# Attention of layer 1 with full-height low-part scores, one burst of value products per unit, and an order of TensorE written in the source

## The chip, the cores and the metric

The kernel runs on one core of one Trainium2 chip. The metric is the device time of one execution in microseconds (us). Five engines run beside each other, each with its own instruction queue: TensorE (PE in the profile, with its weight loads shown as PEld), VectorE (DVE), ScalarE (ACT), GpSimd (POOL) and SyncE (SP, which here only issues transfers). A difference of about 0.2% is the least that a measurement of this kernel can tell from none.

## The reference, cut to what matters

The reference is two transformer blocks in a row, on 512 tokens of width 1024. The first has two layers; the second of these, layer 1, is a windowed attention with 16 query heads of 64 features and 4 heads of keys and values, in which each tile of 128 queries sees its own tile, its neighbours and 256 context keys. The second block has a gated recurrence and a second, banded attention with 8 heads, and then two feed-forward parts. The lines on which the change bears are these:

```python
s_loc = jnp.einsum('bqhgd,bkhd->bhgqk', qb, kb).astype(jnp.float32) * scale
s_loc = jnp.where(valid, s_loc, NEG_INF)
s_ctx = jnp.einsum('bqhgd,bkhd->bhgqk', qb, k_ctx).astype(jnp.float32) * scale
p = jax.nn.softmax(jnp.concatenate([s_loc, s_ctx, s_sink], axis=-1), axis=-1)
return (jnp.einsum('bhgqk,bkhd->bqhgd', p_loc, vb)
        + jnp.einsum('bhgqk,bkhd->bqhgd', p_ctx, v_ctx))
...
scores = jnp.einsum('bnqhd,bnkhd->bnhqk', qc, kb) * (B_HD ** -0.5)
```

Everything is in float32, and the result is held to float32 accuracy.

## The kernel before

**Precision.** Most matrix products are made from operands that are split into a high part and a low part (`split`, L213: ScalarE casts the high part, VectorE or GpSimd subtracts it). A product then takes three passes in the fast matmul type, high by high, high by low and low by high (`mm3`, `gemm_T`, `gen_T`; all of them record on L157). The products of the probabilities with the values and the transposes run on plain float32 (L164 and L169).

**Layer 1.** The attention is cut into 16 units: a part `g` of the queries (four heads, two of each of two key heads) by a tile `i` of 128 queries. A unit goes through four stages:

- `unit_a` (L865) makes the scores. `score` writes one head: a product of the stacked queries `[hi; lo]` with the keys' high part, which `k_stack` has copied to both halves of the partitions, so that 128 rows are used, and then a product of the queries' high part alone (64 rows) with the keys' low part (64 rows of `kxl` or `kcl`). VectorE then adds the mask and takes the maximum (`evac`, L885), and ScalarE takes the exponentials. The scores of an inner tile (`mid`) lie in `sc` (256 context keys, two heads) and `sl` (384 keys of the window); those of an outer tile in one `sl` of 512.
- `trans` (L937) transposes one tile of 128 keys of the four heads on TensorE (`pt`), and ScalarE copies it to SBUF (`pr`).
- `link` (L947) adds one tile of keys to the unit's output `O`. Each product is issued as two halves of 64 output rows (`mm2`, L162), one for each half of the array's columns. With the first tile, four more such halves spread the reciprocal sums (`esk`). With the last tile, VectorE and ScalarE multiply by the gate and split the result (`yt`, `ybh`, `ybl`).
- Between these, `F.pace` issues independent work of TensorE, the fill: the projections of queries and gates (`gt`, L157), in the second half of the units the output product of the first token tiles (`gn`) and the first projections of block 2 (`pn`).

**What sets the order.** The driver (from L1106) walks over `links`, the 72 pairs of a unit and a key tile. Scores run `TL + 5 + SLACK` links ahead and transposes `TL` = 3 links ahead, and each link is followed by 1.0 to 1.2 us of fill (`FP`). This is the order in which the instructions are issued to a scheduler, which then sets the final order of each engine by priorities (`tc.high_priority`) and by when it expects operands to be ready. Only SP's queue is held to the order of the source (`manual_schedule`). Two halves of one product may so be separated by fill.

**Keys.** `k_stack` makes four transfers of 64 rows for each pair of key heads, issued on SP by `move`. They stand in SP's queue between the loads of weights (L234), and the load of the mask (`bmask`) stands behind them. The later `later(us, fn)` issues something once about so much more work of TensorE has been issued.

**Bands.** `band_a` (L1308) scores a head of the second block's banded attention in the same manner: eight products, high parts of 128 rows and low parts of 64 rows (`bk`, `bkl`, to `bS`) by turns, on keys which `band_stack` (L1147) has split and stacked.

**Pools.** PSUM is one pool of eight banks. `SLOTS` gives the number of SBUF tiles of 2 KB per partition under each tag. 24 results are written to DRAM through GpSimd's own queue (`keep`, L676).

Of the kernel before, what the change touches and what calls it, by code (L numbers as in the profile page):

```python
# [9 lines left out]
ALU = mybir.AluOpType  # L10
AX = mybir.AxisListType
P = 128
# [6 lines left out]
SLOTS = {'u': 34, 't': 13, 'p': 7}  # L19
# [3 lines left out]
# Projections of queries and gates for the attention of layer 1 in the order of need: part of the columns,  # L23
# from 4 on for the second half of the tokens.
# [79 lines left out]
def body(tc, I, out, WB=4, RB=4, LOOK=3, RA=2, TL=3, SLACK=1, NA=2, FP=(1.0, 1.2, 1.15, 3.3), HP=(30, 30, 30, 0), BW=(0.64, 0.63, 1.71, 1.5)):  # L104
# [56 lines left out]
    def mm2(ps, l, r, start, stop):  # L161
        """Two products of 64 rows each, in the two column halves of the array at once."""  # L162
# [22 lines left out]
    def settle(fill=None):  # L185
        """Issue all that was put off, with independent work in between as long as there is any."""
# [82 lines left out]
    def gemm_T(w, xparts):  # L269
        """w: per-k (hi, lo) of [128, 128 features]; xparts: (per-k (hi, lo), n) -> psum [128, n]."""  # L270
# [13 lines left out]
    def gen_T(w, xparts, evac, g=2):  # L284
        """gemm_T in steps of g contraction chunks."""
# [13 lines left out]
    class Fill:  # L299
        """Steps of independent tensor work, taken in order between the links of a latency-bound chain."""  # L300
# [17 lines left out]
        def pace(self, us):  # L318
            """Steps worth us of tensor work, less what earlier ones went beyond."""
# [13 lines left out]
    def pause(us):  # L333
        """Lets a chain of this length pass while the main stream goes on."""
# [40 lines left out]
    def ada_rows(b):  # L375
        """Layer 0: shift and scale of chunks 2b, 2b + 1 for cond and cond_ctx, as rows; even k above, odd k below."""
# [29 lines left out]
    def ada_acc(l, nb, conds, fin):  # L406
        """cond @ w for 512 columns as a sum over partitions of what the vector engine adds up, in steps of a slab."""
# [48 lines left out]
    def h_chunks(b, a):  # L456
        """(1 + scale) * x + shift for chunks 2b, 2b + 1; a: [shift | 1 + scale, chunk, cond | cond_ctx]."""
# [102 lines left out]
    def y_ahead(n):  # L560
        """Splits of y for the output product, by pass over its rows and chunk."""
# [63 lines left out]
    def ln_half(ps, gate, res, o, st, h):  # L625
        """o <- ALPHA * res + gate * ps for half h of a token tile; its statistics into st."""
# [149 lines left out]
    def k_stack(z, ks):  # L776
        """ks[e] <- [hi; hi] of head e of a pair, from the pair's hi."""
# [859 lines left out]
```

## Time and profile before

| | |
|---|---|
| median of 3 runs | 1845.38 us (1844.33 to 1846.56) |
| span of the profiled execution | 1844.1 us |
| TensorE busy | 1807.3 us, 98% of the span |
| VectorE busy | 984.6 us, 53% |
| ScalarE busy | 683.9 us, 37% |
| GpSimd busy | 185.2 us, 10% |
| stage of layer 1's units, first score to last value product | 660.8 to 972.4 us |
| stage of the bands, first score to last value product | 1091 to 1274 us |

An engine's busy time is the time in which the profiler shows an instruction on it. Matmuls are pipelined, so the length of one record of TensorE (its second column in the timeline) overlaps with the next; what one costs in a row of them is the distance from its start to the start of the next, and that is how the timeline's rows are used here. A plain float32 product leaves two records, so a row that says x2 is one instruction and x4 is two. TensorE's clock has two levels, 2.4 GHz (1.00 in the column PEclk) and 1.2 GHz (0.50).

### The profile page before, as it was taken

The page shows a single profiled execution, that of the slowest core. Times are in us where ns is not written, and L with a number is a line of the kernel's source. Part 1 is how long each engine was busy: PE and PEld are TensorE (multiplying, and loading weights), DVE is VectorE, ACT ScalarE, POOL GpSimd, SP SyncE. Part 2 cuts the span into 40 slices and gives each one's busy share as a digit, 9 for nine tenths or more (in the row PEclk, how much of TensorE's full clock was granted, in tenths as well). Part 3 has the DMA queues.
Part 4 walks back from the last instruction along what each step waited for, and adds up shares of the span by engine and source line. Part 5 has one row for each costly group of instructions (what it writes and reads, how often), then busy time and mean ns, then how long its engine had stood idle before and what let it go on. Part 6 is the DMA issues. An engine that isn't in the chain of part 4 may idle for free. (4 is left out here: it accounts for less than half of the span.)

```text
span 1844.1 us, 24591 instructions
## 1 busy us (share of the span) xinstructions
PE 1807.3 (98%) x9728; PEld 1455.2 (79%) x9728; DVE 984.6 (53%) x1782; ACT 683.9 (37%) x1275; POOL 185.2 (10%) x144
## 2 busy tenths in 40 slices
PE   8999999999999999999999899999999999999998
PEld 5788888888778987666667777778888888888887
DVE  2335676555565886555666765774445333332253
ACT  2322222222434355455454555423234332322152
POOL 1000000000000221112023611221001000000000
PEclk9999999999999999999999999999999999999999
DMA  8312343324445451222135563211244323233331
GB/s 282 130 57 80 103 142 122 115 92 131 147 148 174 134 160 58 69 81 69 64 109 160 172 205 98 69 63 58 92 136 145 107 93 102 93 99 105 110 99 69
DMA packets 66996, 209.31 MB, mean 114 GB/s; under 512 B 9152, under 2 KB 10176, under 8 KB 66880
## 3 DMA queue, kind: packets, MB, share of 16 engines
q1 hardware_dynamic: 64960, 201.45, 33.8%
q0 software_dynamic: 1920, 6.29, 0.9%
q8 instruction: 76, 1.25, 0.3%
q14 instruction: 40, 0.33, 0.1%
HBM read 195.65 MB, written 8.39 MB: 111 GB/s over the span
## 5 line engine op out<-in xcount | busy, mean ns | idle before, releaser
L214 ACT CAST hi<-raw 128x1024 fp32r<-128x1024 f32 x284 | 298.8, 1053 | 618.1 <-issue 168.4
L215 DVE TENSOR_TENSOR lo<-raw,hi 128x1024 fp32r<-128x1024 f32 x236 | 292.8, 1244 | 360.6 <-ACT hi L214 357.9
L215 POOL TENSOR_TENSOR lo<-raw,hi 128x1024 fp32r<-128x1024 f32 x48 | 117.8, 2459 | 303.0 <-ACT hi L214 302.6
L157 PE MATMUL gt<-hnhl,hi 128*128 128x512 f32 (+1 forms) x384 | 142.7, 372 | 0.2 <-DVE hnhl L199 0.2
L157 PE MATMUL gt<-hnhh,hi 128*128 128x512 f32 (+1 forms) x384 | 142.7, 372 | 0.1
L365 POOL TENSOR_TENSOR rstd<-vr,mhalf 128x1 f32<-128x1 f32 (+2 forms) x40 | 38.6, 966 | 1036.9 <-DVE vr L208 1033.3
L157 PE MATMUL gt<-hnhh,lo 128*128 128x512 f32 (+1 forms) x384 | 142.4, 371 | 0.0
L157 PE MATMUL gt<-hxhh,hi 128*128 128x512 f32 x256 | 104.3, 408 | 0.0
L157 PE MATMUL gt<-hxhh,lo 128*128 128x512 f32 x256 | 101.6, 397 | 0.0
L157 PE MATMUL gt<-hxhl,hi 128*128 128x512 f32 x256 | 101.2, 395 | 0.0
L157 PE MATMUL gt<-h2hh,hi 128*128 128x512 f32 x224 | 90.5, 404 | 0.0
L157 PE MATMUL gt<-h2hh,lo 128*128 128x512 f32 x224 | 87.5, 390 | 0.0
L157 PE MATMUL gt<-h2hl,hi 128*128 128x512 f32 x224 | 87.4, 390 | 0.0
L157 PE MATMUL gt<-h1hh,hi 128*128 128x256 f32 x288 | 86.4, 300 | 0.0
L157 PE MATMUL gt<-h1hl,hi 128*128 128x256 f32 x288 | 85.0, 295 | 0.0
L157 PE MATMUL gt<-h1hh,lo 128*128 128x256 f32 x288 | 83.7, 291 | 0.0
L157 PEld LDWEIGHTS gt<-hnhh,hi 128*128 128x128 f32 x384 | 72.3, 188 | 12.9 <-DVE hnhh L659 0.3
L157 PEld LDWEIGHTS gt<-hnhl,hi 128*128 128x128 f32 x384 | 72.3, 188 | 12.7 <-DVE hnhl L199 0.4
L157 PEld LDWEIGHTS gt<-hnhh,lo 128*128 128x128 f32 x384 | 72.3, 188 | 12.5
L202 DVE SCALAR_TENSOR_TENSOR z<-z,gt 128x256 f32<-128x256 f32 (+1 forms) x48 | 23.3, 505 | 105.8 <-ACT z L211 105.8
L157 PE MATMUL gt<-lc,hi 128*128 128x256 f32 x256 | 71.7, 280 | 0.0
L157 PE MATMUL gt<-hc,lo 128*128 128x256 f32 x256 | 71.6, 280 | 0.0
(373 smaller groups left out, 4205.1 us busy)
## 6 DMA issues: line engine op xcount, KB each, us to landing
raw<-ada_w SPq DMA_DIRECT2D x32, 512.0 KB, 4.4
raw<-a_o SPq DMA_DIRECT2D x32, 512.0 KB, 3.9
raw<-w_fg SPq DMA_DIRECT2D x22, 512.0 KB, 3.8
raw<-w_fu SPq DMA_DIRECT2D x22, 512.0 KB, 3.7
raw<-w_fd SPq DMA_DIRECT2D x22, 512.0 KB, 3.7
raw<-ada SPq DMA_DIRECT2D x16, 512.0 KB, 5.2
raw<-a_v SPq DMA_DIRECT2D x16, 512.0 KB, 4.2
raw<-a_u SPq DMA_DIRECT2D x16, 512.0 KB, 3.8
```

The costliest lines, as they stand in the source:

```text
L157: nc.tensor.matmul(ps, l, r, start=start, stop=stop)
L202: nc.vector.scalar_tensor_tensor(o, a, s, b, op0=o0, op1=o1)
L214: nc.scalar.copy(hi, src)
L215: (eng or nc.vector).tensor_tensor(lo, src, f(hi), op=ALU.subtract)
L365: nc.gpsimd.tensor_tensor(r, t, mhalf[:, :w], op=ALU.pow)
```

## The change

- `k_stack` now stacks the low parts as well as the high parts: a pair of key heads has four stacked tiles (`ks`) and eight transfers, where there were two tiles and four transfers. `score` and `band_a` make the second product over all 128 rows, the stacked queries `[hi; lo]` with `[lo; lo]`; so the product of low by low is now added too.
- In an inner tile, `unit_a` issues the scores of both heads, context and window, before it issues their evacuation.
- `link` becomes `burst`: the four `esk` halves and all of a unit's products with the values are issued without anything between.
- The driver walks over units. Within `manual_schedule` for TensorE it issues, for unit n, the burst, and then the transposes of unit n + 1 and the four steps of the scores of unit n + 2, each followed by an equal share of `FU` = 6.2 us of fill. TensorE's queue keeps this order from the first unit to the last; the other engines are still ordered by the scheduler.
- `SLOTS` grows from 34 to 38 tiles of tag `u` and from 7 to 8 of tag `p`; `dynamic_dma_scratch_size`, the SBUF set aside for GpSimd's queue of transfers, is set to 4096 bytes per partition.
- Comments are replaced by empty lines; up to L775 the line numbers stay the same.

```diff
-SLOTS = {'u': 34, 't': 13, 'p': 7}
+SLOTS = {'u': 38, 't': 13, 'p': 8}
...
-    def k_stack(z, ks):
-        for e, r in enumerate((lo_half, hi_half)):
-            for d in (lo_half, hi_half):
-                move(ks[e][d, :], z[r, :])
+    def k_stack(zs, kk):
+        for z, ks in zip(zs, kk):
+            for e, r in enumerate((lo_half, hi_half)):
+                for d in (lo_half, hi_half):
+                    move(ks[e][d, :], z[r, :])
...
-            es = slice(e * 64, e * 64 + 64)
-            q = qs[a, g][e]
-            qsl = slice(jj * 256 + (i % 2) * P, jj * 256 + (i % 2 + 1) * P)
-            mm(o, q[:, qsl], k[0][e][:, r], True, False)
-            mm(o, q[es, qsl], k[1][es, r], False, True)
+            q = qs[a, g][e][:, jj * 256 + (i % 2) * P:jj * 256 + (i % 2 + 1) * P]
+            mm(o, q, k[0][e][:, r], True, False)
+            mm(o, q, k[1][e][:, r], False, True)
...
-    def link(n, x):
+    def burst(n):
         g, i = units[n]
         Pp, jp = divmod(g, 2)
         keys, ek = pend[n][1:]
         tick()
-        if x == 0:
-            pO_[0] = PS("O")
-            for jj in range(2):
-                r = mm2(pO_[0][:, 256 + jj * P:256 + (jj + 1) * P],
-                        [ek[:, 2 * e + jj:2 * e + jj + 1].to_broadcast([P, 64]) for e in range(2)], [ident] * 2, True, True)
-        pO = pO_[0]
-        v, p_ = vv[keys[x]], pr.pop((n, x))
-        with tc.issue_after(r.ins) if x == 0 else ExitStack():
+        pO = PS("O")
+        for jj in range(2):
+            mm2(pO[:, 256 + jj * P:256 + (jj + 1) * P],
+                [ek[:, 2 * e + jj:2 * e + jj + 1].to_broadcast([P, 64]) for e in range(2)], [ident] * 2, True, True)
+        for x, key in enumerate(keys):
+            v, p_ = vv[key], pr.pop((n, x))
             mm2(pO[:, 0:256], [v[:, (2 * Pp + e) * 64:(2 * Pp + e + 1) * 64] for e in range(2)],
                 [p_[:, e * 256:(e + 1) * 256] for e in range(2)], x == 0, x == len(keys) - 1)
...
+    with tc.manual_schedule(engines={mybir.EngineType.PE}):
+        F.pace(FP[3])
+        for n in range(2):
+            for _ in range(5):
+                a_step(n)
+                F.pace(1.0)
+        for x in keys_of(0):
+            trans(0, x)
+            F.pace(0.6)
+        F.pace(1.5)
+        for n in range(NU):
+            F.until(("b_z", n // 2))
...
+            burst(n)
+            work = []
+            if n + 1 < NU:
+                work += [lambda x=x: trans(n + 1, x) for x in keys_of(n + 1)]
+            work[4:4] = [lambda: a_step(n + 2)]
+            work[2:2] = [lambda: a_step(n + 2)]
+            work[0:0] = [lambda: a_step(n + 2)]
+            work += [lambda: a_step(n + 2)]
+            us = FU[n >= 8] / (len(work) + 1)
+            F.pace(us)
+            for w in work:
+                w()
+                F.pace(us)
+        F.until()
...
-            mm(ps[:, o:o + n], q[es, i * P:(i + 1) * P], kl[es, 0:n], False, True)
+            mm(ps[:, o:o + n], q[:, i * P:(i + 1) * P], kl[e][:, 0:n], False, True)
...
-    nc = bacc.Bacc("TRN2", target_bir_lowering=False, num_devices=1)
+    nc = bacc.Bacc("TRN2", target_bir_lowering=False, num_devices=1, dynamic_dma_scratch_size=4096)
```

The first place is TensorE's queue around the value products of an inner unit of layer 1 (before; `gt` is fill, `O` the unit's output, `pr` a transposed key tile, `v` the values):

```order
L157 MATMUL gt_6556<-h1hh_4289,hi_6317 128x256
L157 MATMUL gt_6556<-h1hl_4290,hi_6317 128x256
L164 MATMUL O_6603<-pr_6525,v_5069 64x256
L157 MATMUL gt_6556<-h1hh_4289,lo_6318 128x256
L164 MATMUL O_6603<-pr_6525,v_5069 64x256
L157 MATMUL gt_6556<-h1hh_4289,hi_6317 128x256
```

And a burst of the changed kernel:

```order
L157 MATMUL gt_6299<-h1hh_4289,lo_6079 128x256
L164 MATMUL O_6336<-ident,esk_6104 64x128 x4
L164 MATMUL O_6336<-pr_6207,v_5079 64x256 x2
L164 MATMUL O_6336<-pr_6222,v_5079 64x256 x2
L164 MATMUL O_6336<-pr_6267,v_5132 64x256 x2
L164 MATMUL O_6336<-pr_6291,v_5132 64x256 x2
L157 MATMUL gt_6299<-h1hh_4289,hi_6078 128x256
```

The two halves of a product, which stood apart with fill between and around them, now stand next to each other, and all products of a unit stand in one run; in the changed order there are 16 such runs, of 12 or 14 instructions.

The second place is TensorE's queue at the scores of an outer tile, one head (before; `kc` and `kx` are high parts of 128 rows, `kcl` and `kxl` low parts of 64 rows):

```order
L157 MATMUL gt_6556<-h1hh_4289,lo_6318 128x256
L157 MATMUL sl_6610<-kc_4911,qy_6141 128x256
L157 MATMUL sl_6610<-kcl_4912,qy_6141 128x256
L157 MATMUL sl_6610<-kx_4906,qy_6141 128x256
L157 MATMUL sl_6610<-kxl_4907,qy_6141 128x256
L157 MATMUL sl_6617<-kc_4911,qy_6141 128x256
```

And after (`ks_4914` and `ks_4906` are high parts, `ks_4916` and `ks_4908` low parts, all of 128 rows):

```order
L157 MATMUL gt_6299<-h1hh_4289,lo_6079 128x256
L157 MATMUL sl_6365<-ks_4914,qx_5807 128x256
L157 MATMUL sl_6365<-ks_4916,qx_5807 128x256
L157 MATMUL sl_6365<-ks_4906,qx_5807 128x256
L157 MATMUL sl_6365<-ks_4908,qx_5807 128x256
L157 MATMUL sl_6372<-ks_4914,qx_5807 128x256
```

The products stay as many and as wide, and each low one now has the height of its neighbours.

The third place is SP's queue ahead of the first unit (before; `raw` is a slab of weights):

```order
L234 DMA raw_5422<-b_q 128x1024
L774 DMA kx_4902<-kz_4908 64x512 x2
L774 DMA kx_4903<-kz_4908 64x512 x2
L774 DMA kx_4905<-kz_4909 64x512 x2
L774 DMA kx_4906<-kz_4909 64x512 x2
L234 DMA raw_5473<-b_q 128x1024
L234 DMA raw_5509<-b_z 128x1024
L150 DMA bmask<-bmask 128x1024
```

And after:

```order
L234 DMA raw_5432<-b_q 128x1024
L774 DMA ks_4902<-kz_4910 64x512 x2
L774 DMA ks_4903<-kz_4910 64x512 x2
L774 DMA ks_4904<-kzl_4911 64x512 x2
L774 DMA ks_4905<-kzl_4911 64x512 x2
L774 DMA ks_4906<-kz_4912 64x512 x2
L774 DMA ks_4907<-kz_4912 64x512 x2
L774 DMA ks_4908<-kzl_4913 64x512 x2
L774 DMA ks_4909<-kzl_4913 64x512 x2
L234 DMA raw_5491<-b_q 128x1024
L234 DMA raw_5527<-b_z 128x1024
L150 DMA bmask<-bmask 128x1024
```

Eight transfers more stand ahead of two slabs of weights and of the mask.

## Rows read from the trace of the kernel before

**Rows 1.** The page's span and its first part: busy time, share of the span and number of instructions of each engine.

```profile
span 1844.1 us, 24591 instructions
PE 1807.3 (98%) x9728; PEld 1455.2 (79%) x9728; DVE 984.6 (53%) x1782; ACT 683.9 (37%) x1275; POOL 185.2 (10%) x144
```

**Rows 2.** Busy time by stretch: the stretch and its length, busy us (and instructions) of PE, PEld, DVE, ACT and POOL, TensorE's granted clock, the DMA engines' share and GB/s. The first row is the stage of the units, the second its first part, the third two microseconds in that, the last the stage of the bands.

```profile
660.80:972.40 311.60, 308.02 (x1741) 211.63 (x1740) 188.16 (x474) 164.65 (x389) 51.20 (x27) 0.99 0.25 79
660.80:690.00 29.20, 27.41 (x159) 21.27 (x157) 24.42 (x61) 16.24 (x35) 7.15 (x3) 0.94 0.40 128
678.00:680.00 2.00, 2.00 (x11) 2.00 (x11) 1.53 (x6) 0.62 (x2) 0.00 (x0) 0.50 0.59 240
600.00:640.00 40.00, 38.62 (x299) 37.34 (x298) 35.90 (x72) 16.42 (x39) 7.46 (x12) 1.00 0.41 134
1010.00:1050.00 40.00, 33.50 (x146) 27.38 (x145) 34.69 (x39) 21.20 (x40) 22.86 (x15) 0.91 0.52 172
1091.00:1274.00 183.00, 176.90 (x1252) 136.57 (x1251) 122.68 (x297) 83.04 (x166) 36.04 (x28) 1.00 0.26 80
```

**Rows 3.** Timeline of TensorE around one value product whose halves stand apart: start, length, engine, line, operation, out<-in, tile of the array, shape, type, records.

```profile
754.38 0.28 PE L157 MATMUL gt<-h1hh,hi 128*128 128x256 f32 x1
754.59 0.65 PE L164 MATMUL O<-pr,v 128*64 128x256 f32 x2
755.17 0.39 PE L157 MATMUL gt<-h1hl,hi 128*128 128x256 f32 x1
755.49 0.65 PE L164 MATMUL O<-pr,v 128*64 128x256 f32 x2
756.06 0.39 PE L157 MATMUL gt<-h1hh,lo 128*128 128x256 f32 x1
756.28 0.28 PE L157 MATMUL gt<-h1hh,hi 128*128 128x256 f32 x1
756.40 0.28 PE L157 MATMUL gt<-h1hl,hi 128*128 128x256 f32 x1
```

**Rows 4.** Timeline of TensorE: value products whose halves stand together, two products in one run (x8) and one product (x4), each with the row behind it.

```profile
689.29 1.03 PE L164 MATMUL O<-pr,v 128*64 128x256 f32 x8
690.25 0.39 PE L157 MATMUL gt<-h1hl,hi 128*128 128x256 f32 x1
...
760.82 0.60 PE L164 MATMUL O<-pr,v 128*64 128x256 f32 x4
761.35 0.38 PE L157 MATMUL sl<-kcl,qx 64*128 64x256 f32 x1
```

**Rows 5.** Timeline of TensorE, the first and the last of the 74 rows of the stage that hold one half of a value product alone (x2; two of them x1). Four further rows hold three halves.

```profile
692.81 0.65 PE L164 MATMUL O<-pr,v 128*64 128x256 f32 x2
...
971.62 0.65 PE L164 MATMUL O<-pr,v 128*64 128x256 f32 x2
```

**Rows 6.** Timeline of TensorE within the scores of one outer tile: low and high parts by turns.

```profile
758.64 0.38 PE L157 MATMUL sl<-kcl,qx 64*128 64x256 f32 x1
758.95 0.39 PE L157 MATMUL sl<-kx,qx 128*128 128x256 f32 x1
759.26 0.38 PE L157 MATMUL sl<-kxl,qx 64*128 64x256 f32 x1
```

**Rows 7.** Timeline of TensorE, the first and the last of the 128 rows of the stage with a product of 64 rows.

```profile
660.99 0.38 PE L157 MATMUL sl<-kcl,qx 64*128 64x256 f32 x1
...
938.47 0.38 PE L157 MATMUL sl<-kxl,qy 64*128 64x256 f32 x1
```

**Rows 8.** Timeline of TensorE, the scores of one head of the bands, eight products of 128 to 512 columns: the first of them, and the row behind the last.

```profile
1091.47 0.22 PE L157 MATMUL bS<-bk,qx 128*128 128x128 f32 x1
...
1094.10 0.50 PE L157 MATMUL gt<-h2hh,hi 128*128 128x512 f32 x1
```

**Rows 9.** Groups of VectorE's and ScalarE's instructions by line and shape from 690 to 930 us: the evacuation of the scores, the exponentials and the copies of the transposes, with the count, the busy us, the mean ns of one, and the idle time before them and its releaser.

```profile
L885 DVE CUSTOM_DVE_ANT_0 tsl<-sl,bmask,mc 128x384 f32<-128x384 f32 x28 | 17.2, 616 | 4.2 <-PE sl L157 2.9
L885 DVE CUSTOM_DVE_ANT_0 tsc<-sc,bmask,sink 128x256 f32<-128x256 f32 x28 | 13.5, 482 | 24.3 <-PE sc L157 24.2
...
L945 ACT COPY pr<-pt 128x512 f32<-128x512 f32 x58 | 31.7, 589 | 65.9 <-PE pt L169 65.9
L211 ACT ACTIVATE tsl<-tsl,nmx 128x384 f32<-128x384 f32 x30 | 18.1, 604 | 0.0
L211 ACT ACTIVATE tsc<-tsc,nmx 128x256 f32<-128x256 f32 x30 | 15.0, 500 | 5.4 <-DVE nmx L206 5.3
```

**Rows 10.** Timeline of SP's queue ahead of the first unit: the transfers of stacked keys, and the mask's.

```profile
647.12 7.00 SPq L774 DMA_DIRECT2D kx<-kz  x8
...
655.29 0.42 SPq L150 DMA_DIRECT2D bmask<-bmask  x1
```

**Rows 11.** Issues of transfers from 600 to 700 us: out<-in, engine, count, KB each, median us from issue to landing.

```profile
xd<-xn POOLq DMA_DIRECT2D x8, 256.0 KB, 2.5
...
bmask<-bmask SPq DMA_DIRECT2D x1, 512.0 KB, 6.9
```

**Rows 12.** Timeline of GpSimd, the first and the last row of the eight writes to DRAM ahead of layer 1's units.

```profile
626.55 0.75 POOL L676 DMA_DIRECT2D xd<-xn  x1 [10.20 <-DVE xn L199]
...
638.25 0.54 POOL L676 DMA_DIRECT2D xd<-xn  x1 [1.14 <-DVE xn L199]
```

**Rows 13.** Timeline of TensorE, the largest idle time of the stage's first part and what ended it.

```profile
676.41 0.38 PE L157 MATMUL sc<-kc,qx 128*128 128x256 f32 x1 [1.79 <-DVE mc L885]
```

More of the change, by code (lines that the diff above doesn't have):

```diff
@@ L774, in move, with k_pair @@
         nc.sync.dma_start(f(o), f(i))
-    def k_stack(z, ks):
-        for e, r in enumerate((lo_half, hi_half)):
-            for d in (lo_half, hi_half):
-                move(ks[e][d, :], z[r, :])
+    def k_stack(zs, kk):
[3 more added lines that the diff above has]
+                    move(ks[e][d, :], z[r, :])
+    def k_pair():
+        return tuple((R("ks"), R("ks")) for _ in range(2))
     def q_stack(src):
@@ L788, in q_stack @@
         return x, y
-    kx = [((R("kx"), R("kx")), R("kxl")) for _ in range(2)]
-    kz = [R("kz"), R("kz")]
-    kc = ((R("kc"), R("kc")), R("kcl"))
-    kcz = R("kcz")
+    kx = [k_pair(), k_pair()]
+    kz = [(R("kz"), R("kzl")) for _ in range(2)]
+    kc = k_pair()
+    kcz = (R("kcz"), R("kczl"))
     for m in range(2):
@@ L898, in unit_a @@
                 pc, t = PS("sc"), T("tsc", tag="t")
-                for j in pair:
-                    o = slice(j % 2 * 256, (j % 2 + 1) * 256)
+                half = [slice(j % 2 * 256, (j % 2 + 1) * 256) for j in pair]
+                for j, o in zip(pair, half):
                     score(pc[:, o], j, kc, cs)
+                pls = [PS("sl") for _ in pair]
+                for j, pl in zip(pair, pls):
+                    score(pl[:, 0:384], j, kx[Pp], ks)
+                for j, o in zip(pair, half):
                     evac(t[:, o], pc[:, o], P, sink[j], col(mc)[j])
                     parts.append([t[:, o]])
-                for j in pair:
-                    pl, t = PS("sl"), T("tsl", tag="t")
-                    score(pl[:, 0:384], j, kx[Pp], ks)
+                for j, pl in zip(pair, pls):
+                    t = T("tsl", tag="t")
                     evac(t[:, 0:384], pl[:, 0:384], 5 * P, col(mc)[j], col(mx)[j])
@@ L1105, in body @@
     pend = {}
-    F.pace(FP[3])
-    links = [(n, x) for n in range(16) for x in range(4 if units[n][1] in (0, 3) else 5)]
-    first_ = {n: g for g, (n, x) in reversed(list(enumerate(links)))}
-    a_steps = [(first_[n] - TL - 5 + k - SLACK, n) for n in range(16) for k in range(5)]
-    ga = {}
-    nt = 0
-    for g in range(-TL - 5 - SLACK, len(links)):
-        while a_steps and a_steps[0][0] <= g:
-            n = a_steps.pop(0)[1]
-            if n not in ga:
-                F.until(("b_q", n // 2))
-                ga[n] = unit_a(n, *units[n])
-            next(ga[n], None)
-        while nt < min(len(links), g + 1 + TL):
-            with tc.high_priority(offset=90):
-                trans(*links[nt])
-            nt += 1
-        n = links[max(g, 0)][0]
-        F.pace(FP[0] if g < 0 else FP[1] if n < 8 else FP[2])
-        if g < 0:
-            continue
-        if n < 15 and g == first_[n + 1] - 1 or n == 15:
-            F.until(("b_z", n // 2))
-        if g == first_[8]:
-            lr1.extend(ln_rows(1))
-            F.add(out_b((0, 1)), "o")
-            for nme, q in QZ[14:]:
-                F.add(proj[nme](256, q % 4), (nme, q))
-            F.add(pause(0))
-            F.add(projN("w_qb", pn["w_qb"], (0, 1)))
-            F.add(projN("w_kb", pn["w_kb"], (0, 1)))
-        with tc.high_priority(offset=30):
-            link(*links[g])
@@ L1139, in body, with a_step, keys_of @@
-    F.until()
+    NU = len(units)
+    steps = {}
+    def a_step(n):
+        if n < NU:
+            if n not in steps:
+                F.until(("b_q", n // 2))
+                steps[n] = unit_a(n, *units[n])
+            next(steps[n], None)
+    def keys_of(n):
+        return range(4 if units[n][1] in (0, 3) else 5)
+    with tc.manual_schedule(engines={mybir.EngineType.PE}):
[9 more added lines that the diff above has]
+        for n in range(NU):
+            F.until(("b_z", n // 2))
+            if n == 8:
+                lr1.extend(ln_rows(1))
+                F.add(out_b((0, 1)), "o")
+                for nme, q in QZ[14:]:
+                    F.add(proj[nme](256, q % 4), (nme, q))
+                F.add(pause(0))
+                F.add(projN("w_qb", pn["w_qb"], (0, 1)))
+                F.add(projN("w_kb", pn["w_kb"], (0, 1)))
+            burst(n)
[12 more added lines that the diff above has]
+        F.until()
```

35 lines of the change are left out of this document (17 added, 18 removed).

## The prediction

> **What bounds the kernel now.** I read the engines' shares first: TensorE is busy for 98% of the span, so nothing else can bound the time much [rows 1]. Then the stretches: in the stage of layer 1's units TensorE is busy for 308.0 of 311.6 us at a clock of 0.99, VectorE for 188.2 and ScalarE for 164.7; in the stage of the bands TensorE for 176.9 of 183.0 us [rows 2]. There is next to no idle time to win. What can be won is in the busy time, and for that the timeline has to be read by the distances between starts. Fill products of 256 columns follow each other at 0.12 us (756.28 to 756.40) [rows 3]. Two things break this pace.
>
> *Value products whose halves stand apart.* From 754.38 to 756.28 us TensorE does three fill products and the two halves of one value product, in 1.90 us [rows 3]. Each half holds it for 0.58 us. A product whose halves stand together holds it for 0.53 us, both halves included, and two such products in one run for 0.96 us [rows 4]; a further product in a run so costs 0.43 us. Two neighbouring halves thus run side by side, and a half alone costs as much as the pair, 0.43 us. The rest is the change between products on the whole array and products on half its columns: 1.90 - 3 x 0.12 - 2 x 0.43 = 0.68 us for four changes, 0.17 us each.
>
> *Low parts of 64 rows.* Where they stand by turns with products of 128 rows, every start is 0.31 us from the last, where 0.12 is due [rows 6]: 0.19 us for each change of height.
>
> **The change part by part.**
>
> *Value products in a burst.* The order of before has 78 halves of a value product alone and 33 pairs, which the trace bears out (74 rows with one half and four with three, so 78) [rows 5]; of the `esk` halves, half as wide, 6 stand alone and 29 pairs together. Afterwards there are 72 and 32 pairs. Before: (78 + 33) x 0.43 + (6 + 29) x 0.215 = 55.3 us; after: 72 x 0.43 + 32 x 0.215 = 37.8. That saves 17.4 us.
>
> *Changes of the array's shape.* Counted along the order of before there are 198 between the whole array and half columns, 214 between 128 and 64 rows (for the 128 low products [rows 7]), and 18 directly between the two narrow shapes, which I price at 0.18. That is 198 x 0.17 + 214 x 0.19 + 18 x 0.18 = 77.6 us. Afterwards there are 16 bursts and no product of 64 rows: 32 x 0.17 = 5.4 us. That saves 72.2 us. A low product over 128 rows is priced like its neighbour of high parts, at 0.12 us for 256 columns; the evacuation reads the same tiles as before. Together TensorE's work in the units falls by 89.6 us, from 308.0 to 218.4. All of it lies on the path, since TensorE is the engine that sets the end.
>
> On 64 rows there is a rule of the Trainium skill that speaks the other way: TensorEngine Tiling (Array Packing), section When to Use Tiling, has contractions of up to 64 rows use half the rows, with two such products side by side. By that, paired low parts of two heads would take half of 128 x 0.12 to 0.18 us, some 9 us less than the full height now chosen. The rows above decide it here: a low product in this order has a neighbour of 128 rows and runs alone.
>
> *Bands.* One head's eight products take 2.63 us up to the next row [rows 8]; by width, at 0.12 us for 256 columns, they are worth 2 x (0.06 + 0.12 + 0.18 + 0.24) = 1.20. Eight heads: 8 x 1.43 = 11.4 us of TensorE's work goes.
>
> *More transfers of keys on SP.* Eight took 7.0 us of issue time ahead of the units [rows 10]; sixteen take 14. Behind them stand two slabs and the mask, which moves from 655.3 to 662.3 us and lands 6.9 us after its issue [rows 11], at 669. VectorE's first evacuation needs it. That is where the first units were slow already: 1.79 us of idle time for VectorE's release of PSUM [rows 13]. I put this at 0 to 7 us, once. The 16 transfers more at the bands and four at the context keys are issued well ahead of their readers, beside TensorE's fill: nothing.
>
> *Smaller scratch of GpSimd's queue.* Eight writes were issued within 12 us [rows 12], with 2.5 us to landing [rows 11]. If each had to wait for the one before, they would take 8 x 2.5 = 20, and the slabs' low parts behind them on GpSimd would be 8 us late. No row shows such a wait, so I take nothing and keep 8 us for the range. The larger pools cost nothing; they only give the scheduler more room.
>
> *TensorE's order fixed.* This is the edit that can cost. Whatever waits now holds all of TensorE's queue behind it: the fill too. Take unit 3, an inner one. By the changed order, between its last scores and its first transposes stand 48 fill products (5.8 us), a burst (2.5) and eight scores (1.0), over 9 us with eight transposes of the unit before not counted. Beside that run its evacuation on VectorE, 2 x (0.48 + 0.62), its exponentials on ScalarE, 4 x (0.50 + 0.60), and one copy of 0.59 [rows 9]: 7.2 us if nothing else is in these queues. So the pipeline is deep enough, by 2 us, if the queues are short. But the queues get fuller: the same 188 us of VectorE and 165 us of ScalarE now stand against 218 us of TensorE, 86% and 75%, where they stood against 308. How much TensorE loses at that load, no row shows for this order. Three stretches bound it [rows 2]. From 600 to 640 us VectorE is busy for 90%, and TensorE loses 1.4 us to 38.6 of work, 4%. From 660.8 to 690 (VectorE 84%, the same work as here) it loses 1.8 us idle and, at a clock of 0.94, 1.6 more, to 25.8 of work: 13%. From 1010 to 1050 (VectorE 87%, a chain of norms) it loses 6.5 us idle and 3.0 by a clock of 0.91, to 30.5: 31%. On 218 us that is 9, 28 and 68 us. I take the middle one, whose row is the start of this very stage. The clock belongs to it: after the idle time of 1.79 us TensorE was granted 0.50, the lower of its two levels, from 678 to 680 us [rows 2, 13], so a wait can cost again about as much as it lasted.
>
> **The sum.** The units go from 311.6 to 218.4 + 28 = 246 us, 65 less. Of the bands' 11.4 us I count 7, since their recurrence on VectorE and ScalarE already leaves TensorE 6 us idle there; 0 and 11.4 bound it. The sum is 72 us: from 1844.1 to 1772 us in the profile, which stands 1.3 us below the median of the runs, so 1773.5.
>
> **The rivals.**
>
> *The cover holds.* TensorE loses only 9 us in the units and nothing in the bands: 1845.4 - (311.6 - 227) - 11.4 = 1749 us. For it speaks that no link of the chain is longer than the 9 us of cover; against it the load of VectorE. Chance 0.14.
>
> *VectorE and ScalarE become the bound.* TensorE gets ahead of the evacuation, PSUM's eight banks fill, and it waits as it did around 1010 to 1050 us: 68 us lost in the units, 4 of 11.4 won in the bands: 1845.4 - (311.6 - 286) - 4 = 1816 us. It decides where VectorE's queue adds over 2 us to most units' chains. The Trainium skill states this outcome as a rule, in TensorEngine Tiling (Array Packing), section PSUM Bottleneck: a faster TensorE does not evacuate PSUM any faster. Chance 0.20, from 1795 us on.
>
> *The chain is laid bare.* If the fixed order put a unit's transposes ahead of what they need by the length of the whole chain, each of 16 units would lose its 7.2 us and the lower clock behind it about 1.6 more: 141 us against 101 won, 1885 us, slower than before. It decides from 6.3 us lost per unit (101 / 16). The order speaks against it, with its 9 us of cover; a scheduler's order of VectorE in which an evacuation stands behind something late would speak for it. Chance 0.03.
>
> *It doesn't do what it says.* If halves in a long burst ran one after the other, 72 x 0.43 = 31 us would come back, 1804 us; the run of two products at 0.96 us speaks against it [rows 4]. If the changes of shape cost nothing and the distances had another reason, the time would stay: 1845. Chance 0.02.
>
> **How the numbers follow.** The forecast, 1755 to 1795 us, has 0.61; the cover that holds 0.14, VectorE's bound 0.20, the bare chain 0.03, no effect 0.02. The range of 1748 to 1812 us takes in most of the first three. Faster by over 0.2%, about the least that a measurement of this kernel can tell from no change: 0.61 + 0.14 + 0.20 = 0.95; same 0.02; slower 0.03.
>
> **What would show it.** Runs of 12 or 14 half-column instructions, a further product at 0.43 us each; scores at 0.12 us with no row of 64 rows; TensorE's busy time from first score to last value product near 220 to 235 us; idle time of TensorE before `pt` and `sc`/`sl` rows released by ScalarE and VectorE, some 15 us with the clock at 0.50 behind the longer ones. The prediction is wrong if the scores of 128 rows take over 0.12 us, if TensorE's idle time there is over 50 us, or if the stretches outside the two stages move by more than some us.

## The result and the profile after

The changed kernel takes 1762.32 us (median of 4 runs, 1760.37 to 1764.6); the kernel before took 1845.93 us beside it. The ratio is 0.9542, with a 95% interval of 0.9523 to 0.9562: 84 us less. The forecast was 1773.5 us, 72 less; the time lies in its range, 11 us below the likeliest value.

Page of the changed kernel, the span and the engines' shares, as in [rows 1]:

```profile
span 1759.8 us, 24646 instructions
...
PE 1710.9 (97%) x9728; PEld 1437.0 (82%) x9728; DVE 975.0 (55%) x1782; ACT 680.7 (39%) x1275; POOL 186.8 (11%) x144
```

Busy time by stretch of the changed kernel, columns as in [rows 2]: the units from first score to last value product; from first score to the first score of the bands; the units in three parts; the rest:

```profile
662.25:908.07 245.82, 236.38 (x1800) 206.23 (x1800) 188.38 (x484) 171.37 (x404) 60.19 (x32) 0.99 0.35 115
662.25:1013.40 351.15, 333.80 (x2236) 285.94 (x2237) 262.39 (x573) 227.23 (x501) 102.93 (x55) 0.98 0.42 137
662.25:695.00 32.75, 26.89 (x198) 24.31 (x198) 26.05 (x65) 21.45 (x46) 7.42 (x3) 0.93 0.54 180
695.00:830.00 135.00, 133.80 (x1067) 119.94 (x1064) 103.98 (x279) 92.81 (x218) 28.98 (x12) 0.99 0.30 98
830.00:914.00 84.00, 81.62 (x570) 66.91 (x569) 62.14 (x147) 60.46 (x149) 24.83 (x17) 1.00 0.34 114
1013.40:1759.00 745.60, 731.64 (x3857) 606.80 (x3855) 339.09 (x577) 258.06 (x446) 45.12 (x44) 1.00 0.31 101
```

The same view of the kernel before, cut at its first score of the bands:

```profile
660.78:1091.47 430.69, 418.82 (x2238) 302.06 (x2237) 271.45 (x576) 229.10 (x502) 102.53 (x55) 0.99 0.34 108
1091.47:1844.00 752.53, 740.52 (x3857) 607.39 (x3855) 341.19 (x573) 258.36 (x446) 45.39 (x44) 1.00 0.30 98
```

The units' stretch alone can't be compared, since in the changed order some 59 records of later work have moved into it (1800 against 1741). Cut at the bands' first score, TensorE's records are the same but for two (2236 and 2238). So the two spans are compared in three pieces:

| stretch | before | after | difference |
|---|---|---|---|
| start to first score | 660.78 | 662.25 | +1.5 |
| first score to first score of the bands | 430.69 | 351.15 | -79.5 |
| from there to the end of the span | 752.6 | 746.4 | -6.2 |

In the second piece TensorE's busy time fell by 85.0 us (418.82 to 333.80), and its idle time grew by 5.5 (11.87 to 17.35). In the third its busy time fell by 8.9 us and its idle time grew by 2.0 (12.01 to 13.96). The gain is in the busy time, and VectorE's and ScalarE's work stayed nearly the same.

Timeline of TensorE in the changed kernel, columns as in [rows 3]: the scores of one head pair in an outer tile, one burst, and one head of the bands, each with the row behind it:

```profile
701.13 1.12 PE L157 MATMUL sl<-ks,qy 128*128 128x256 f32 x8
702.09 0.28 PE L157 MATMUL gt<-h1hh,hi 128*128 128x256 f32 x1
...
833.28 0.66 PE L164 MATMUL O<-ident,esk 128*64 128x128 f32 x8
833.76 2.33 PE L164 MATMUL O<-pr,v 128*64 128x256 f32 x20
836.02 0.50 PE L157 MATMUL gn<-hi,ybh 128*128 128x512 f32 x1
...
1013.40 1.44 PE L157 MATMUL bS<-ks,qx 128*128 128x128 f32 x8
1014.67 0.40 PE L157 MATMUL gt<-h2hh,hi 128*128 128x512 f32 x1
```

Eight scores now take 0.96 us, 0.12 each as forecast, where each took 0.31 [rows 6]; another eight, at 823.42 us, take 1.06. Five value products (x20: ten halves, two records each) take 2.26 us, 0.45 each, where one product whose halves stood apart took 1.90 together with three fill products [rows 3]. A head of the bands takes 1.27 us instead of 2.63 [rows 8].

What TensorE waited for in the units of the changed kernel: waiting operation and line, releaser and line, us in total, times, longest:

```profile
PE O L164 <- ACT pr L950: 2.5, 2, 2.2
PE pt L169 <- ACT tsc L211: 2.3, 3, 0.8
PE pt L169 <- DVE mc L887: 1.4, 1, 1.4
PE sl L157 <- DVE qx L199: 1.2, 1, 1.2
PE sl L157 <- DVE mx L887: 1.1, 1, 1.1
PE sc L157 <- DVE z L202: 1.0, 1, 1.0
```

The three longest within the units, with their times, from the timeline of TensorE (the bracket is the idle time and its releaser):

```profile
672.67 1.58 PE L157 MATMUL sl<-ks,qx 128*128 128x384 f32 x4 [1.14 <-DVE mx L887]
683.81 0.77 PE L169 MATMUL pt<-ident,tsl 128*128 128x128 f32 x4 [1.38 <-DVE mc L887]
693.79 1.73 PE L164 MATMUL O<-pr,v 128*64 128x256 f32 x8 [2.15 <-ACT pr L950]
```

Of the units' waits, all of over 0.8 us stand in the first 33 us. There TensorE is idle for 5.9 us; from 695 to 830 us it loses 1.2 us of 135, and from 830 to 914 us 2.4 of 84. The wait for `qx` is the one ahead of the first score. Behind two of the waits TensorE was granted its lower clock, in the first and the third row here; behind the 1.38 us at 683.81 it was not (the second row). The last row, at 950 us, is the third stretch at the lower clock between the first score and the bands:

```profile
673.60:677.00 3.40, 3.40 (x16) 3.40 (x16) 3.40 (x8) 0.00 (x0) 2.31 (x1) 0.50 0.35 125
...
684.00:686.00 2.00, 2.00 (x18) 1.84 (x17) 2.00 (x10) 1.93 (x6) 0.00 (x0) 1.00 0.63 231
...
694.10:697.50 3.40, 3.40 (x17) 2.47 (x14) 1.56 (x2) 1.60 (x3) 0.00 (x0) 0.50 0.00 0
...
950.10:956.90 6.80, 3.95 (x14) 3.47 (x15) 4.78 (x10) 3.70 (x7) 4.44 (x5) 0.50 0.43 154
```

The changed kernel was profiled a second time (`after_again` below). There the same wait for `pr` was not followed by the lower clock, and only one stretch of the three came back, at 948 us:

```profile
693.39 1.13 PE L164 MATMUL O<-pr,v 128*64 128x256 f32 x8 [2.32 <-ACT pr L950]
```

```profile
662.54:1011.57 349.03, 330.87 (x2237) 283.31 (x2237) 261.85 (x573) 227.35 (x501) 102.87 (x55) 0.99 0.42 138
694.10:697.50 3.40, 3.40 (x29) 3.04 (x26) 2.92 (x7) 1.72 (x2) 0.97 (x1) 1.00 0.07 19
948.00:954.80 6.80, 3.72 (x13) 3.34 (x14) 4.77 (x12) 3.47 (x7) 4.21 (x5) 0.50 0.42 154
```

So the two profiles of one kernel differ by the clock: 10.8 us of TensorE's busy time stood at the lower level in the first and 3.7 in the second, and the first is busy for 2.9 us more. That is about 0.42 us lost for each us at the lower level. It has to be taken out before busy times of single profiles are compared; the table behind the experiments does that.

SP's queue in the changed kernel, the mask's transfer:

```profile
662.44 0.42 SPq L150 DMA_DIRECT2D bmask<-bmask  x1
```

The mask's issue moved by 7.2 us, as forecast, from 655.29 [rows 10] to 662.44.

### The profile page after: what moved, and what is told of

Its sections match the earlier page's. It is cut to its first block, busy times and chain, and to the rows that moved or that the text cites. A ratio compares the mean times of both kernels' runs of the same rounds, so it can differ in the third digit from the quotient of the medians.

```text
span 1759.8 us, 24646 instructions
## 1 busy us (share of the span) xinstructions
PE 1710.9 (97%) x9728; PEld 1437.0 (82%) x9728; DVE 975.0 (55%) x1782; ACT 680.7 (39%) x1275; POOL 186.8 (11%) x144
## 4 chain that ended last, share of the span: by engine, by line
PE 50%; DVE 4%; issue 2%; ACT 2%; POOL 1%; SPq 0%; DMA 0%; POOLq 0%; DVEq 0%; ACTq 0%
PE gt L157 25%; PE gn L157 13%; PE pn L157 4%; PE O L164 1%; PE pt L169 1%; PE sl L157 1%; POOL rstd L365 1%; PE pp L157 1%; PE bp L1366 1%; ACT tsl L211 1%; PE lv L164 1%; PE tr L169 1%; PE bO L164 1%; PE bS L157 1%; PE hO L157 0%
```

## The experiments

Unless said otherwise, a kernel is the changed one with the edit shown, the gap is from first score to first score of the bands, and "busy" is TensorE's.

**Low parts on 64 rows again.** The low parts are no longer stacked, so a pair of key heads has four transfers again. All else stays: bursts, the fixed order, the pools.

```diff
-            mm(o, q, k[1][e][:, r], False, True)
+            mm(o, q[es, :], k[1][es, r], False, True)
...
-            mm(ps[:, o:o + n], q[:, i * P:(i + 1) * P], kl[e][:, 0:n], False, True)
+            mm(ps[:, o:o + n], q[es, i * P:(i + 1) * P], kl[es, 0:n], False, True)
```

> The changed kernel with the low parts of the keys back on 64 rows, in the units and in the bands; burst and fixed order stay. Each of the 128 low products of the units then stands alone between products of 128 rows. Theory A (a change of the array's shape costs TensorE 0.17 to 0.19 us): 256 changes more in the units, 49 us, and 64 in the bands, 11 us: 1762 + 60 = 1822 us, some us less where waits of the changed kernel are filled. Theory B (the gain is the fixed order and the burst, the height hardly matters): under 1775 us.

Measured: 1805.28 us (1801.64 to 1808.15), ratio 0.9776 (0.976 to 0.9792). Its timeline, and its gap by stretch:

```profile
717.39 0.39 PE L157 MATMUL sc<-ks,qy 128*128 128x256 f32 x1
717.71 0.38 PE L157 MATMUL sc<-kczl,qy 64*128 64x256 f32 x1
718.02 0.44 PE L157 MATMUL sl<-ks,qy 128*128 128x384 f32 x1
```

```profile
660.63:1047.69 387.06, 376.53 (x2238) 295.25 (x2237) 266.27 (x577) 226.77 (x502) 101.16 (x55) 0.99 0.35 120
```

The 0.31 to 0.32 us from start to start are back. Busy time is 42.7 us more than in the changed kernel for 256 changes of height, 0.17 us each (0.18 at equal clock); idle time is 6.8 us less. So 43 us of the kernel's gain of 84 (1805.28 against 1762.32) are the low parts' height, and a slower TensorE hides a part of the waits.

**The same with half as many changes:** two high products, then their two low ones; for this the scores of both heads of an outer tile are issued ahead of their evacuation.

```diff
             mm(o, q, k[0][e][:, r], True, False)
-            mm(o, q[es, :], k[1][es, r], False, True)
+            lows.append((o, q[es, :], k[1][es, r], False, True))
+            if len(lows) == 2:
+                for l in lows:
+                    mm(*l)
+                lows.clear()
```

> As the kernel before in this list, but two high products are issued and then their two low ones, so that as many products of 64 rows need half as many changes of height. Theory A: 128 changes more in the units (24 us) and 32 in the bands (6 us) than in the changed kernel: 1762 + 30 = 1792 us. Rival A2 (a product of 64 rows is slow by itself, not the change): the same 1822 us as with the low parts alone.

Measured: 1778.16 us (1777.03 to 1779.54), ratio 0.9636 (0.9622 to 0.965). Its gap:

```profile
658.64:1025.84 367.20, 354.56 (x2238) 287.86 (x2237) 260.64 (x577) 226.37 (x502) 102.47 (x55) 0.98 0.37 126
```

The products are the same as in the run before, and 64 rows high. Busy time is 20.8 us over the changed kernel for 128 changes, 0.16 us each (0.17 at equal clock). What costs is the change, not the product of 64 rows (the two low ones of a pair lie on the same 64 rows, so they are not two that share the array).

**Low parts of 128 rows alone,** in the kernel before, with the larger pools and the smaller scratch, without burst or fixed order.

```diff
-            mm(o, q[es, qsl], k[1][es, r], False, True)
+            mm(o, q[:, qsl], k[1][e][:, r], False, True)
```

> The kernel before with only the low parts stacked to 128 rows, in units and bands, and the room (38 and 8 tiles, scratch of 4096) that this needs; links, scheduler's order and halves apart as before. Theory A: its TensorE order has 216 changes of shape where there were 430, 42 us less in the units and 11 in the bands: 1846 - 53 = 1793 us. Theory B (order and burst make the gain): 1835 us or more, the bands' part alone.

Measured: 1811.58 us (1808.52 to 1812.51), ratio 0.9814 (0.9799 to 0.9829). Its gap, and the start of it:

```profile
661.28:1064.44 403.16, 382.62 (x2227) 294.29 (x2225) 270.63 (x572) 228.66 (x501) 102.82 (x55) 0.97 0.35 119
...
661.28:695.00 33.72, 24.77 (x165) 22.37 (x164) 27.15 (x67) 20.28 (x44) 7.09 (x3) 0.85 0.48 162
```

Its largest waits:

```profile
670.19 1.01 PE L157 MATMUL sl<-ks,qx 128*128 128x384 f32 x2 [3.49 <-DVE z L202]
...
682.06 0.58 PE L157 MATMUL sc<-ks,qx 128*128 128x256 f32 x1 [5.29 <-DVE mc L888]
```

Busy time fell by 36.2 us, but idle time grew by 8.7 (11.87 to 20.54). Two waits at the stage's start make up 8.8 us, and the clock there is 0.85. In the whole gap 19.1 us of the work stood at the lower clock, against 7.5 in the kernel before; at equal clock busy time fell by some 41 us, where 42 were expected (some 1 us of it because 11 records fewer stand in this gap). So the price was right, and a part of it was lost at the stage's start. This part alone gains 34 us and the rest of the change alone (the first run) 40; together they gain 84; no run takes the 10 us over their sum apart.

**The order of TensorE not fixed.** The same issue order, left to the scheduler, run in two sets; in the second the changed kernel ran beside it.

```diff
-    with tc.manual_schedule(engines={mybir.EngineType.PE}):
+    with ExitStack():
```

> The changed kernel without the fixed order of TensorE: the same source order of bursts, transposes, scores and fill, handed to the scheduler. Its TensorE queue still has 17 runs of half-column products. Theory A: 1762 us, within 6. Theory C (holding TensorE to the source's order is itself what gains, since the scheduler guesses readiness wrongly): 1785 us or more. Theory D (the fixed order costs waits that the scheduler would avoid): 1750 us or less.

> The changed kernel without the fixed order of TensorE, once more beside the changed kernel itself. If the fixed order costs some waits that the scheduler's order avoids: 4 us less than the changed kernel, 1758 us. If the difference of the single comparisons was noise between chips: the same within 1 us.

> The changed kernel as it is, as the measure for the two runs beside it on the same chip: 1762 us.

Measured: 1757.87 us (1756.24 to 1759.5), ratio 0.9526 (0.9511 to 0.954), and in the second set 1758.98 us (1758.06 to 1759.32), ratio 0.953 (0.9517 to 0.9543), beside 1760.08 us (1759.61 to 1764.94), ratio 0.9542 (0.9529 to 0.9555), of the changed kernel. The intervals overlap. In the second set all four times without the fixed order lie below all four with it, but the medians are 1 us apart, less than can be told from none here. The fixed order brings nothing by itself: what gains is the order in which the source issues the bursts, which the scheduler keeps whole but for one (17 runs of half-column products instead of 16).

**The products of a burst spread,** halves together, each product followed by fill that is taken from the rest of the unit.

```diff
-            burst(n)
+            sums, prods, gate = burst_parts(n)
+            sums()
+            for p_ in prods:
+                p_()
+                F.pace(0.6)
+            gate()
```

> The changed kernel with the value products of a unit no longer in one run: the two halves of a product stay together, but 0.6 us of fill follows each product as long as there is fill. 112 changes between whole and half columns where there were 32. Theory A: 80 x 0.17 = 14 us more, 1776 us. Theory B2 (what gains is that halves stand together, the length of the run doesn't matter): 1762 to 1765 us.

Measured: 1780.67 us (1777.52 to 1781.92), ratio 0.9643 (0.9629 to 0.9658). One product in its timeline, and its gap:

```profile
737.70 0.28 PE L157 MATMUL gt<-h1hh,lo 128*128 128x256 f32 x1
737.91 0.65 PE L164 MATMUL O<-pr,v 128*64 128x256 f32 x4
738.49 0.39 PE L157 MATMUL gt<-h1hh,hi 128*128 128x256 f32 x1
738.71 0.28 PE L157 MATMUL gt<-h1hl,hi 128*128 128x256 f32 x1
```

```profile
662.15:1033.82 371.67, 348.99 (x2237) 285.82 (x2237) 263.55 (x573) 226.67 (x501) 101.84 (x55) 0.97 0.39 129
```

From the first row to the fourth pass 1.01 us, of which the products are 2 x 0.12 and 0.43: 0.34 for two changes, 0.17 each. Busy time is 15.2 us more for 80 more changes, of which some 2 us are the clock (15.9 us of the work at the lower level, against 10.8), which leaves 0.16 each; idle time is 5.3 us more. So the run of products gains by its fewer changes, apart from what the neighbouring halves gain.

**The halves of a burst apart:** first all upper halves, then all lower ones, without fill between.

```diff
-            mm2(pO[:, 0:256], [v[:, (2 * Pp + e) * 64:(2 * Pp + e + 1) * 64] for e in range(2)],
-                [p_[:, e * 256:(e + 1) * 256] for e in range(2)], x == 0, x == len(keys) - 1)
...
+        for e in (1, 0):
+            o = pO[64 * e:64 * e + 64]
...
+            for x, key in enumerate(keys):
+                nc.tensor.matmul(o[:, 0:256], vv[key][:, (2 * Pp + e) * 64:(2 * Pp + e + 1) * 64],
+                                 ps_[x][:, e * 256:(e + 1) * 256], start=x == 0, stop=x == len(keys) - 1)
```

> The changed kernel, but each burst issues all its upper halves first (64 columns of the array, the other head's left empty) and then all its lower halves; same products, same number of changes of shape, no fill between. Theory G, two neighbouring halves run side by side and so cost 0.43 us for the pair, while halves of the same columns run one after the other: the 72 products cost 72 x 0.43 = 31 us more and the esk halves 32 x 0.215 = 7 more, 38 us, less some us of waits that the slower pace absorbs: 1795 to 1800 us. Rival H, halves cost the same wherever they stand and the gain of the burst came from the changes of shape alone: 1762 us, no difference.

Measured: 1782.91 us (1781.73 to 1783.73), ratio 0.966 (0.9646 to 0.9673); 22.8 us over the changed kernel beside it. One burst of five products:

```profile
809.69 0.65 PE L963 MATMUL O<-ident,esk 128*64 128x128 f32 x4
810.18 1.67 PE L967 MATMUL O<-pr,v 128*64 128x256 f32 x7
811.48 0.43 PE L963 MATMUL O<-ident,esk 128*64 128x128 f32 x2
811.69 0.38 PE L967 MATMUL O<-pr,v 128*64 128x256 f32 x1
811.75 0.38 PE L963 MATMUL O<-ident,esk 128*64 128x128 f32 x2
811.90 2.38 PE L967 MATMUL O<-pr,v 128*64 128x256 f32 x12
814.22 0.50 PE L157 MATMUL gn<-hi,ybh 128*128 128x512 f32 x1
```

It takes 4.53 us, against 2.74 in the changed kernel (833.28 to 836.02). From 810.18 to 811.69 stand seven records of upper halves, 0.22 us each, so 0.43 for a half of two records: a half among halves of its own columns costs as much as a pair of neighbours (0.45). But the first lower halves already start while the last upper ones run (811.48 to 811.90), which the expectation of 38 us had left out: by it this burst should take 2.58 us longer, and it takes 1.79. Busy time in the gap is 25.4 us more than in the run beside it:

```profile
660.34:1032.33 371.99, 356.24 (x2237) 302.26 (x2237) 266.66 (x573) 228.05 (x501) 101.58 (x55) 0.99 0.39 129
```

That neighbouring halves run side by side is shown; of the 38 us put on it here, 25 are there.

**More load on VectorE:** three products of 512 columns per unit that nothing reads.

```diff
             burst(n)
+            for _ in range(3):
+                tt(dump, dump, dump, ALU.mult)
```

> The changed kernel with three multiplications of 128x512 on VectorE added to each unit, whose result nobody reads: about 2 us a unit, 33 us in all, so that VectorE's share in the units rises from 76% to about 89%. Theory E (loss follows VectorE's load, as the prediction had it): TensorE loses about 15 us or more besides, 1780 us or more. Theory F (the loss is the filling of the pipeline at the start of the stage and single waits; the cover of over 9 us holds): 1762 to 1770 us.

Measured: 1765.5 us (1763.89 to 1766.95), ratio 0.9563 (0.9549 to 0.9578). The middle of its units by stretch:

```profile
695.00:830.00 135.00, 128.12 (x1008) 113.04 (x1007) 124.15 (x307) 90.32 (x212) 30.12 (x12) 0.99 0.28 94
```

VectorE is busy there for 92% instead of 77%, and TensorE loses 6.9 us idle instead of 1.2. The whole costs 3 us against the changed kernel's first set of runs and 5 against its second. So the load does cost something, 5% of this stretch at 92%, but far less than the 15 us or more that were expected if TensorE's loss followed it.

**The mask ahead of the keys:** mask and sink loaded before the stacked keys are moved.

```diff
     for t in (4, 5):
         vproj(t)
+    msk = load(I["bmask"], [P, 1024], "bmask")
+    snk = C([P, 16], "snk")
+    nc.sync.dma_start(snk, I["b_sink"].partition_broadcast(P))
     settle()
```

> The changed kernel with the loads of the mask and of the sink issued on SP ahead of the projections of the keys, so that they don't stand behind the 16 transfers of stacked keys. Theory G (the first units wait because the mask comes 7 us later): the idle time from 660 to 695 us falls by 3 to 6 us, 1756 to 1759 us. Theory H (they wait for the chain of evacuation and exponentials, the mask is there in time): 1761 to 1764 us.

Measured: 1760.99 us, ratio 0.9539 (0.952 to 0.9558), no difference that can be measured. The median is that of all four runs; three took 1760.05 to 1761.45 us, and one 4966.37, for which nothing here gives a reason. The 7 us on SP's queue cost nothing.

**The pools and the scratch alone,** in the kernel before.

```diff
-SLOTS = {'u': 34, 't': 13, 'p': 7}
+SLOTS = {'u': 38, 't': 13, 'p': 8}
...
-    nc = bacc.Bacc("TRN2", target_bir_lowering=False, num_devices=1)
+    nc = bacc.Bacc("TRN2", target_bir_lowering=False, num_devices=1, dynamic_dma_scratch_size=4096)
```

> The kernel before with only the larger pools (38 and 8 tiles) and the scratch of 4096 bytes. If the smaller scratch makes GpSimd wait for its transfers: up to 8 us more, 1854 us. If more tiles let the scheduler do better: some us less. My theory: neither, 1846 us within 3.

Measured: 1845.82 us (1843.75 to 1850.7), ratio 0.9998 (0.9988 to 1.0007). Both edits are worth nothing here.

**More work ahead of the first burst,** in the kernel with the order not fixed and the mask early.

```diff
-        F.pace(1.5)
+        F.pace(4.0)
         for n in range(NU):
...
-def body(..., FU=(6.2, 6.2)):
+def body(..., FU=(5.8, 6.2)):
```

> The changed kernel without the fixed order of TensorE, with the mask loaded ahead of the stacked keys and 4.0 instead of 1.5 us of fill ahead of the first burst, taken from the fill of the first eight units (5.8 instead of 6.2 us each). Theory I, what TensorE still loses in this stage sits in the filling of the pipeline at its start, in waits for single evacuations, and more work ahead of the first burst covers a part of it: 1 to 4 us less than the run without the fixed order, 1754 to 1757 us. Rival J, the waits move to another place with the fill that is taken away: the same 1758 us or more.

Measured: 1764.61 us (1763.12 to 1766.78), ratio 0.9559 (0.9546 to 0.9572): 5.6 us slower than the second run without the fixed order (1758.98), which has the mask late, a difference that was worth nothing in its own run. Its start and one of its later waits:

```profile
663.94:697.00 33.06, 29.16 (x232) 26.86 (x232) 30.21 (x75) 24.01 (x49) 9.09 (x4) 1.00 0.49 171
```

```profile
800.38 1.09 PE L169 MATMUL pt<-ident,tsl 128*128 128x128 f32 x8 [1.76 <-DVE mx L887]
```

The idle time at the start is no shorter for it: 3.9 us of these 33.1, against 4.0 of 34.3 without it. The clock there is whole, but so it is at the start of the changed kernel's second profile. The first score came 3.3 us later (663.94 against 660.68), and more waits came up further on, where fill had been taken away; idle time in the gap is 21.2 us against 17.1. The time is as the rival had it, and the theory is not borne out. No version was found that is shown to beat the changed kernel by more than can be told from none.

**The busy times at equal clock.** For each profile, TensorE's busy time in the gap, how much of it stood at the lower clock (the sum over the windows with 0.50), and the busy time less 0.42 us for each of these:

| profile | busy | of it at 0.50 | at equal clock | changes more |
|---|---|---|---|---|
| kernel before | 418.8 | 7.5 | 415.7 | |
| changed kernel | 333.8 | 10.8 | 329.3 | |
| low parts on 64 rows | 376.5 | 3.5 | 375.0 | 256 of height than the changed kernel: 0.18 us each |
| half as many changes | 354.6 | 9.1 | 350.7 | 128 of height: 0.17 |
| low parts of 128 rows alone | 382.6 | 19.1 | 374.6 | 214 fewer of shape than the kernel before: 0.19 |
| products spread | 349.0 | 15.9 | 342.3 | 80 to half the columns: 0.16 |

## Why the prediction was right, and where it was off

**The price list held.** 89.6 us of TensorE's work were to go; 85.0 went, and 86.4 at equal clock. Each of its three terms has its run: a change of height at 0.17 to 0.18 us by two runs (forecast 0.19, and 0.19 to 0.20 by the rows of the first), a change to half the columns at 0.16 (forecast 0.17), and neighbouring halves at 25 us for a whole set of bursts, where the full sum would have been 38. Why the mean per change of height is a little below what a single row shows stays open. That a lone half between fill costs as much as a pair was assumed from two rows; the run with the halves apart shows it for halves among their own kind.

The Trainium skill states in TensorEngine Tiling (Array Packing), section Key Properties, that a change of the tiling mode drains TensorE, without a price. The runs agree that a change costs by itself: with half as many changes and the same products, half of the cost was gone. That it is a drain, no run here shows.

**The wrong step is the loss of 28 us in the units.** Counted as the prediction did (the units' 311.6 us less the 79.5 won, against 218.4 of work), the loss was 13.7 us, between its bounds of 9 and 28. Of these, 4.6 are work that the price list had taken away and that stayed (1.4 of it the clock); the idle time is 9.1 (3.6 before, and 5.5 more). So the two errors partly offset each other, and the forecast's distance of 11 us is smaller than the error in the loss. Against the sum it is 14.5 us more gain; less the 0.8 by which the bands fell short and the 1.5 by which the first score came later, it gives the 12 us between the sum and the spans (72 and 84.3). The step took the loss of the stage's first 29 us, 13%, and laid it on the whole stage, with VectorE's load as the link. The loss did not spread: the first part lost more than before (5.9 us idle of 32.75, where it was 1.8 of 29.2), but the next 135 us lost 1.2. And the load was set too high: 86% is VectorE's 188 us against TensorE's work of 218, while the rows that it was compared with are shares of elapsed time; against the forecast's own 246 us it is 76%, and 77% was measured from 695 to 830 us, below all three rows. At 92%, in the run with more load, TensorE was idle for 5% of that stretch, near the 4% of the row from 600 to 640 us that the prediction put aside.

Where the loss stands is shown, and the releasers of its waits. That it is the filling of the pipeline, paid once, is argued from the place; the one run that put more work ahead of the first burst did not shorten it, so the reason for this loss stays open.

**VectorE did not become the bound.** The rival at 1816 us, and with it the rule that a faster TensorE evacuates PSUM no faster (the Trainium skill, TensorEngine Tiling (Array Packing), section PSUM Bottleneck), would have come in where an evacuation's queue is longer than the cover. The cover of over 9 us per unit that the prediction counted in the issue order was enough; in the units the waits for VectorE's evacuations (`mc`, `mx`) add up to 2.5 us. No run here reached the point from which the rule decides.

**The rest.** The bands and what follows gave 6.2 us of the 7 counted: 8.9 us of busy time went, where 11.4 were listed, and idle time grew by 2.0. The first score came 1.5 us later, which the prediction did not have: TensorE now waits 1.2 us for `qx` ahead of it. The mask moved by 7.2 us and cost nothing, the low end of the range, as the run with the mask ahead shows; the pools and the scratch cost nothing either. The lower clock came behind two of the longer waits in one profile of the changed kernel and behind none of the units' waits in the other. TensorE idled 9.4 us in the units, where 15 were expected. The fixed order, which was taken to be the edit that can cost, costs at most some us and gains nothing by itself.

## What to carry to other kernels

Where a busy engine is the bound, look in its timeline for starts that lie further apart than the work between them is worth, and count the changes of the array's shape: here each cost 0.16 to 0.20 us, about as much as a product and a half of 256 columns, so a product made twice as high can be cheaper than one that breaks the row. Issue the half-column products of a unit as neighbours and in one run. When the bound engine gets faster, don't spread the loss of a stage's start over the whole stage: here 5.9 of 9.4 us of idle time stood in its first 33 us. Take a helper's load as a share of the time that the stage will last, and compare it with rows that are shares of the same kind: TensorE lost 1.2 us of 135 with the helper at 77%, and 6.9 at 92%. Before busy times of two profiles are compared, look how much of each stood at the lower clock.

## What was not expected of the hardware

Runs of upper and of lower halves overlap where they meet: in the run with the halves apart, the lower halves' first products start 0.4 us before the last of the upper ones (811.48 to 811.90 us), although the upper ones were all issued first.

A wait is not followed by the lower clock each time: 1.14 us (at 672.67) and 2.15 us (at 693.79) were, with 0.50 behind them; 1.38 us (at 683.81) was not, with 1.00 behind it. In the second profile of the same kernel 2.32 us at the same place (693.39) was not either.
